# A four-layer decoder trunk on one core: TensorE in the order of emission, attention in batches

## The chip, the core and the metric

The kernel runs on one core of one Trainium2 chip. The metric is the device time of one execution in microseconds. The core has a matrix engine (TensorE, in the profile PE, with its weight loads as PEld), a vector engine (VectorE, DVE), a scalar engine (ScalarE, ACT), GpSimd (POOL) and SyncE (SP), which here issues DMAs. Each engine runs its own queue of instructions in order; semaphores tie the queues together.

## The reference

256 tokens of width 1024 go through four layers. Each layer is a token mixer and a SwiGLU feed-forward network (FFN, hidden width 2816), and each of these is wrapped in a norm before and a norm after:

```python
for i in range(DEPTH):                       # 4
    kind = i % 3
    hn = rms_norm(x, norm_gains[i, 0])
    if kind == 0:    m = diff_attention(hn, ...)            # layers 0 and 3
    elif kind == 1:  m = stick_breaking_attention(hn, ...)  # layer 1
    else:            m = sliding_window_sink_attention(hn, ...)  # layer 2
    x = x + rms_norm(m, norm_gains[i, 1])
    f = swiglu(rms_norm(x, norm_gains[i, 2]), w_gate[i], w_up[i], w_down[i])
    x = x + rms_norm(f, norm_gains[i, 3])
```

Differential attention (8 heads, rotary positions) takes two softmaxes per head, subtracts lambda times the second from the first, multiplies with the values and norms each head. Stick-breaking attention (16 heads) has sigmoids and a running product in the place of softmax. The third is attention in a window of 128 tokens with 16 query heads, 2 key heads, rotary positions and a learned sink per head. All data are float32.

## The kernel before

**Two streams.** The 256 tokens are two blocks of 128, stream 0 and stream 1 (`s`). Both run the same program, `stream(s)`, a Python generator: for each layer `pre_norm`, the mixer (`layer_a`, `layer_b` or `layer_c`), `out_proj`, `post_norm`, `pre_norm`, `ffn`, `post_norm`. A weight is read from memory once and used by both streams.

**Weight units.** The weights are cut into 378 units of 128 x 1024 numbers. A unit is loaded to a `stage` tile by a DMA on SP, then split into a high part `hi` (ScalarE) and a low part `lo` (VectorE). Every product with a weight is three matmuls of 512 columns: high with high, high with low, low with high. A unit is six such matmuls for each stream (twelve of half the width in layer 2). `RING` = 11 split units are kept; stream 0 may be at most `LAG` = 8 units ahead of stream 1; splits run `AHEAD` = 3 units ahead of stream 0. At an edge (the end of the input projection of a layer, and the end of an FFN) stream 1 goes first as long as stream 0 is past the edge and it is not.

**The emission.** The class `Emitter` runs the two streams and a list of tasks as generators and decides in which order their instructions are written down. It keeps a clock of its own, `em.t`, which goes on with each matmul by its columns times `COLUMN_NS` (four times for float32 products and transposes). A generator that yields `("d", n)` is not run again before n ns have passed on this clock; `("e", key)` waits for an event that another has set; `("w",)` takes the next weight unit. Tasks go first, then stream 0, then stream 1. If nothing can run, the clock jumps to the next time.

**Attention as tasks.** `project` multiplies a chunk (four units) of q, k or v. Each q or k chunk spawns a task `turned`: rotate (VectorE; in `layer_b` a copy on ScalarE), transpose on TensorE, copy to SBUF. After k it goes on as `scores`: two steps of score products, softmax or its like, then transposes of the weights. The task `values` multiplies with V and splits the result for `out_proj`, which waits for an event per head. A layer has two groups `g` of heads (layer 2 four tasks `heads`). In the FFN the task `turn` sends the hidden block through a transposing DMA on SP, with a copy on GpSimd before and after it (`by_dma`, `words`).

**PSUM.** Each stream has one bank tagged `tp` (transposes, values, every other FFN chunk), one tagged `mm`, and two tagged `acc` (scores, `out_proj`, the FFN's sum).

**What sets the order on the chip.** The framework's scheduler orders each engine's queue from its own forecast of times, with the order of emission as priority. Wrapped by `Start`, an instruction can be pinned behind the one before it on its engine. In the kernel before, this holds for ScalarE, VectorE, GpSimd and TensorE only up to stream 1's first norm:

```python
            if i == 0 and s:
                scalars()
                act.on = dve.on = pool.on = pe.on = False
```

Nearly all instructions carry line 182 in the profile, which is the line of this wrapper; they are told apart by tile names: `mm_f` (FFN products), `acc_f`, `acc_a`, `acc_b`, `acc_c` (sums of the FFN's second product and of `out_proj`), `mm_a000q` (layer 0, group 0: the q chunk of stream 0, from the letter of the layer, its number, the stream, the group), `tt_` (transposed q and k), `t_` (the rotated chunk), `sc_` (scores), `tw_`, `ta_`, `tpr_` (transposed weights), `pv_` (values), `to_` (transposed values), `tp_n` and `tp_q` (transposed x for the mixer's and the FFN's norm), `xh_`, `xl_` (its high and low part), `hTh_f` (high part of the transposed hidden block).

Of the kernel before, what the change touches and what calls it, by code (L numbers as in the profile page):

```python
# [38 lines left out]
COLUMN_NS = 1.0 / 2.4  # L39


class Emitter:

# [5 lines left out]
    def __init__(self, load_dma, split, n_units, edges):  # L49
        self.t = 0.0  # L50
        self.load_dma, self.split, self.n, self.edges = load_dma, split, n_units, edges
        self.issued = self.loaded = 0
        self.pos = [0, 0]
        self.ring = {}
        self.events = set()
        self.limit = 0
        self.tasks = []

# [17 lines left out]

    def run_task(self, task):
        while True:
            try:
                what = task[1].send(None)  # L80
            except StopIteration:
                return False
            if what[0] == "d":
                task[0] = self.t + what[1]
                return True
            if what[0] == "e" and what[1] not in self.events:
                task[2] = what[1]
                return True
# [35 lines left out]
    def run(self, gens):  # L124
        mains = [dict(s=s, gen=g, ready=0.0, want=None, done=False) for s, g in enumerate(gens)]
        while True:
            self.advance()
            ran = False
            for task in list(self.tasks):
                if task[2] is not None and task[2] in self.events:  # L130
                    task[2] = None
                if task[2] is None and task[0] <= self.t:
                    if not self.run_task(task):
                        self.tasks.remove(task)
                    ran = True
                    break
            if ran:
                continue

            behind = any(self.pos[1] < w <= self.pos[0] for w in self.edges)  # L140
            order = mains[::-1] if behind else mains
            if self.pos[1] == 0:
                order = sorted(order, key=lambda m: m["want"] is not None)
            for m in order:
                if self.can(m) and m["ready"] <= self.t:
                    self.run_main(m)
                    ran = True
                    break
            if ran:
                continue  # L150
            times = [x[0] for x in self.tasks if x[2] is None] + [m["ready"] for m in mains if self.can(m)]
            if not times:
                assert all(m["done"] for m in mains) and not self.tasks, "the emission is stuck"
                return
            self.t = max(self.t, min(times))
# [3 lines left out]
def trunk_kernel(ctx, tc, x, positions, norm_gains, a_w_in, a_w_out, a_lambda, a_subln, b_w_in, b_w_out,  # L159
# [9 lines left out]
    def bank(tag, s, shape, name):  # L169
        return ps.tile(shape, F32, tag=f"{tag}{s}", name=name, bufs=BANKS[tag])  # L170
# [415 lines left out]
    def layer_a(s, i, xn):  # L586
# [7 lines left out]
        def turned(chunk, g, which):  # L594
            t = rope(chunk, 8, *tabs[which], f"{name}{g}{which}")
            yield ("d", 2000)
# [3 lines left out]
            else:  # L600
                dst = qT[g] = queries(s, 4, f"{name}{g}")
            four_transposes(s, t.rearrange("p h d -> p (h d)"), dst, f"tt_{name}{g}{which}")
# [4 lines left out]
        def scores(g):  # L607
# [3 lines left out]
            yield ("d", 700)  # L611
# [4 lines left out]
            for step in range(3):  # L616
                if step < 2:
# [21 lines left out]
                    yield ("d", 3500)  # L639
                if step > 0:  # L640
                    if step == 2:
                        yield ("d", 1500)
# [5 lines left out]
                    yield ("d", 300)  # L648
# [4 lines left out]
        def values(g):  # L653
# [3 lines left out]
            yield ("d", 500)  # L657
# [12 lines left out]
            yield ("d", 4200)  # L670
# [4 lines left out]
            yield ("d", 900)  # L675
# [3 lines left out]
        for g in range(2):  # L679
            for which in "qkv":  # L680
                chunk = yield from project(s, xn, 512, 4, f"{name}{g}{which}", g == 0 and which == "q")
                if which == "v":
# [4 lines left out]
                    yield ("d", 600)  # L687
                else:
                    em.spawn(turned(chunk, g, which))
                    yield ("d", 1500)  # L690
        return oT, name

    def layer_b(s, i, xn):
# [6 lines left out]
        def turned(chunk, g, which):  # L700
            t = wk.tile([P, 512], F32, tag="t2k", name=f"t_{name}{g}{which}", bufs=TMP)
            act.activation(t, chunk, AF.Copy, scale=xn[2])
            yield ("d", 900)
# [3 lines left out]
            else:  # L707
                dst = qT[g] = queries(s, 4, f"{name}{g}")
            four_transposes(s, t, dst, f"tt_{name}{g}{which}")
# [4 lines left out]
        def scores(g):  # L714
# [3 lines left out]
            yield ("d", 700)  # L718
            aT[g] = wk.tile([P, 4, 2, nk, P], F32, tag=f"wT{s}", name=f"aT_{name}{g}", bufs=1)
            as_ = {}  # L720
            for step in range(3):
                if step < 2:
# [21 lines left out]
                    yield ("d", 3500)  # L744
                if step > 0:
                    if step == 2:
                        yield ("d", 1500)
                    for p in range(2):
                        tp = bank("tp", s, [P, 2, nk, P], f"ta_{name}{g}{2 * step - 2 + p}")
# [4 lines left out]
                        yield ("d", 300)  # L754
            em.set((name, "w", g))

        def values(g):
# [3 lines left out]
            yield ("d", 500)  # L761
# [7 lines left out]
            yield ("d", 900)  # L769
# [3 lines left out]
        for g in range(2):  # L773
            for which in "qkv":
                chunk = yield from project(s, xn, 512, 4, f"{name}{g}{which}", g == 0 and which == "q")
                if which == "v":
# [4 lines left out]
                    yield ("d", 600)  # L781
                else:
                    em.spawn(turned(chunk, g, which))
                    yield ("d", 600)
        return oT, name

    def layer_c(s, i, xn):
# [6 lines left out]
        def keys(chunk):  # L794
# [4 lines left out]
            yield ("d", 1200)  # L799
# [7 lines left out]
        def heads(chunk, g):  # L807
            t = rope(chunk, 4, *tabs["q"], f"{name}{g}q")
            yield ("d", 1300)
# [8 lines left out]
            yield ("d", 700)  # L818
# [24 lines left out]
            yield ("d", 6000)  # L843
            for p in range(2):
                tp = bank("tp", s, [P, 2, nk, P], f"tpr_{name}{g}{p}")
# [4 lines left out]
                yield ("d", 500)  # L850
# [7 lines left out]
            yield ("d", 600)  # L858
# [3 lines left out]
        for part in range(5):  # L862
# [5 lines left out]
            yield ("d", 2000)  # L868
        return oT, name

    def ffn(s, i, xn):
# [19 lines left out]
        def turn(c, h):  # L891
# [7 lines left out]
            split_rows(hT[c], slice(2 * (c % 2), 2 * (c % 2) + 2), t)  # L899
            em.set((name, "h", c))  # L900
# [19 lines left out]
        yield ("d", 700)  # L920
# [3 lines left out]
    def stream(s):  # L924
        if s:
            yield ("d", 1500)
        for i in range(depth):
            kind = i % 3
            xn = pre_norm(s, 4 * i, f"n{i}{s}")
            yield ("d", 600)  # L930
            if i == 0 and s:
                scalars()
                act.on = dve.on = pool.on = pe.on = False
# [4 lines left out]
            yield ("d", 4000)  # L938
            gain = gain_of(i, 3)
            xn = pre_norm(s, 4 * i + 2, f"q{i}{s}")  # L940
            yield ("d", 600)
            acc = yield from ffn(s, i, xn)
            post_norm(s, acc, gain, f"e{i}{s}")
            if i < depth - 1:
                yield ("d", 4000)
# [30 lines left out]
```

## Time and profile before

| | us |
|---|---|
| median of 3 runs | 1189.72 (1189.0 to 1190.4) |
| the profiled execution | 1188.92 |
| its span, first to last instruction | 1187.1 |
| PE busy | 1165.9 (98%) |
| PEld busy | 958.5 (81%) |
| DVE busy | 784.4 (66%) |
| ACT busy | 651.9 (55%) |
| POOL busy | 214.3 (18%) |

The rows that follow in the prediction come from four views. The page starts with the span and each engine's busy time. The view by stretches gives, for each stretch of the span, its length, the busy time and number of instructions of PE, PEld, DVE, ACT and POOL, the granted TensorE clock, the share of the DMA engines and GB/s. The view of waits says which instruction's engine was idle until which other was done: total us, number of times, longest. The view in order of time has start, duration, engine, line, operation, output tile and input tiles, shapes, how many were merged, and in brackets the engine's idle time before it with its releaser. Matmuls are pipelined: the next one starts before the last one's shown end.

### The profile page before, as it was taken

To read this page: it belongs to the slowest core of one execution; us is meant where nothing else is said; L and a number is where in the kernel's file an instruction comes from. 1 tells how busy PE (TensorE), PEld (TensorE's weight loads), DVE (VectorE), ACT (ScalarE), POOL (GpSimd) and SP (SyncE) were. 2 spreads that over 40 slices of the span, in tenths; PEclk is the share of its full clock that TensorE was granted. 3 is DMA by queue.
4 is the path that set the end of the run, shared out by engine and by line. 5 is a ranking of instruction groups with operands and counts; after the bars stand their busy time and mean duration, and the time that the engine had idled before them with its cause. 6 is when DMAs were issued, how large, how long until landed. Compare 5 with 4: busy or idle time off the path is not lost.

```text
span 1187.1 us, 16727 instructions
## 1 busy us (share of the span) xinstructions
PE 1165.9 (98%) x5868; PEld 958.5 (81%) x5868; DVE 784.4 (66%) x1217; ACT 651.9 (55%) x1197; POOL 214.3 (18%) x301
## 2 busy tenths in 40 slices
PE   8999999999999999999999999999999999999997
PEld 7787788888878878888888878888878788888886
DVE  7876665665847666665688666566586785666563
ACT  6665554444756655444476655445475565545442
POOL 2000132222200013222210013221210001322221
PEclk9999999999999999999999999999999999999999
DMA  7635467776743546777764246777765454677761
GB/s 280 212 122 161 146 189 222 209 213 199 239 143 125 178 143 185 216 219 209 200 214 141 90 147 195 213 210 210 207 214 154 137 175 128 177 213 214 208 194 41
DMA packets 184360, 216.41 MB, mean 182 GB/s; under 512 B 53074, under 2 KB 148436, under 8 KB 184276
## 3 DMA queue, kind: packets, MB, share of 16 engines
q1 hardware_dynamic: 183568, 215.00, 61.1%
q8 instruction: 46, 0.75, 0.3%
q10 hardware_dynamic: 708, 0.34, 0.1%
q14 instruction: 38, 0.31, 0.1%
HBM read 203.76 MB, written 1.05 MB: 173 GB/s over the span
## 4 chain that ended last, share of the span: by engine, by line
PE 90%; DVE 3%; ACT 3%; DMA 2%; issue 2%; POOL 1%; ACTq 0%; POOLq 0%; DVEq 0%; SPq 0%
PE mm_f L182 39%; PE acc_f L182 19%; PE acc_a L182 3%; PE mm_c L182 2%; PE acc_b L182 2%; PE sc_a L182 2%; PE acc_c L182 2%; DMA stage<-in_a_w_in_dram 1%; ACT hi L182 1%; DVE lo L182 1%; PE sc_c L182 1%; PE sc_b L182 1%; PE pv_a L182 1%; DVE x L182 1%; PE tp_q L182 1%
## 5 line engine op out<-in xcount | busy, mean ns | idle before, releaser
L182 DVE TENSOR_TENSOR lo<-stage,hi 128x1024 fp32r<-128x1024 f32 x378 | 459.7, 1226 | 162.0 <-ACT hi L182 159.9
L182 ACT ACTIVATE hi<-stage 128x1024 fp32r<-128x1024 f32 x378 | 394.9, 1056 | 163.3 <-PE mm_f L182 86.9
L182 PE MATMUL mm_f<-hi,xh_q 128*128 128x512 f32 x704 | 275.7, 392 | 1.5 <-ACT hi L182 1.5
L182 PE MATMUL mm_f<-lo,xh_q 128*128 128x512 f32 x704 | 274.2, 389 | 0.0
L182 PE MATMUL mm_f<-hi,xl_q 128*128 128x512 f32 x704 | 217.2, 390 | 0.4 <-DVE xl_q L182 0.4
L182 POOL COPY hp_f<-h_f 128x512 uint16<-128x512 uint16 x80 | 90.6, 1132 | 407.7 <-DVE h_f L182 393.7
L182 PEld LDWEIGHTS mm_f<-hi,xh_q 128*128 128x128 f32 x704 | 132.1, 188 | 30.5 <-ACT hi L182 3.2
L182 PEld LDWEIGHTS mm_f<-hi,xl_q 128*128 128x128 f32 x704 | 132.2, 188 | 28.7 <-DVE xl_q L182 1.2
L182 PEld LDWEIGHTS mm_f<-lo,xh_q 128*128 128x128 f32 x704 | 132.3, 188 | 26.9
L182 ACT ACTIVATE hTh_f<-hx_f 128x256 fp32r<-128x256 f32 x80 | 33.4, 418 | 166.8 <-POOL hx_f L182 166.8
L182 PE MATMUL acc_f<-hi,hTh_f 128*128 128x512 f32 x352 | 111.5, 393 | 1.2 <-ACT hTh_f L182 1.2
L182 PE MATMUL acc_f<-hi,hTl_f 128*128 128x512 f32 x352 | 109.8, 390 | 0.0
L182 PE MATMUL acc_f<-lo,hTh_f 128*128 128x512 f32 x352 | 109.8, 390 | 0.0
L182 DVE TENSOR_TENSOR hTl_f<-hx_f,hTh_f 128x256 fp32r<-128x256 f32 x80 | 33.9, 424 | 106.0 <-ACT hTh_f L182 106.0
L182 POOL COPY hx_f<-hq_f 128x512 uint16<-128x512 uint16 x80 | 81.0, 1013 | 85.6 <-DMA hq_f<-hp_f 85.1
L182 ACT ACTIVATE t_f<-mm_f,half_f 128x256 f32<-128x256 f32 x88 | 41.5, 472 | 74.4 <-PE mm_f L182 74.4
L182 PEld LDWEIGHTS acc_f<-hi,hTh_f 128*128 128x128 f32 x352 | 65.8, 188 | 15.5 <-ACT hTh_f L182 2.3
L182 PEld LDWEIGHTS acc_f<-lo,hTh_f 128*128 128x128 f32 x352 | 66.1, 188 | 13.8
L182 PEld LDWEIGHTS acc_f<-hi,hTl_f 128*128 128x128 f32 x352 | 66.0, 188 | 13.7
L182 DVE SCALAR_TENSOR_TENSOR t_f<-t_f,mm_f 128x256 f32<-128x256 f32 x88 | 36.8, 418 | 32.5 <-ACT t_f L182 32.4
L182 DVE SCALAR_TENSOR_TENSOR h_f<-t_f,hsq_f,mm_f 128x256 f32<-128x256 f32 x88 | 42.3, 480 | 2.9
L182 ACT ACTIVATE e_a<-sc_a,nm_a 128x128 f32<-128x128 f32 (+1 forms) x64 | 26.0, 420 | 17.0 <-DVE nm_a L182 16.9
(588 smaller groups left out, 1552.3 us busy)
## 6 DMA issues: line engine op xcount, KB each, us to landing
stage<-in_ffn_w_gate_dram SPq DMA_DIRECT2D x176, 256.0 KB, 3.0
stage<-in_ffn_w_up_dram SPq DMA_DIRECT2D x176, 256.0 KB, 3.3
stage<-in_ffn_w_down_dram SPq DMA_DIRECT2D x88, 512.0 KB, 4.4
stage<-in_a_w_in_dram SPq DMA_DIRECT2D x48, 512.0 KB, 4.4
stage<-in_b_w_in_dram SPq DMA_DIRECT2D x24, 512.0 KB, 4.1
stage<-in_a_w_out_dram SPq DMA_DIRECT2D x16, 512.0 KB, 3.5
stage<-in_c_w_in_dram SPq DMA_DIRECT2D x10, 512.0 KB, 4.4
gain<-in_norm_gains_dram SPq DMA_DIRECT2D x8, 512.0 KB, 4.3
```

Of the source, the lines that this page charges most:

```text
L182: i = call(*args, **kw)
```

## The change

- TensorE stays pinned to the order of emission for the whole program; the other engines are left to the scheduler as before.
- `COLUMN_NS`, the clock's cost of a matmul column, goes from 1/2.4 to 0.443 ns. Nearly all delays are new, most of them longer.
- Tasks run in batches: once no task can run any more, the next one may only run `BATCH_NS` = 2600 ns later.
- A task yields `("b", s)` before it takes a `tp` bank. If the bank of this stream was taken less than `BANK_NS` = 1200 ns ago, the task is put off until then.
- The hidden block's event in `turn` is set 1500 ns later.

No arithmetic, tile or DMA is added or removed.

```diff
-COLUMN_NS = 1.0 / 2.4
+COLUMN_NS = 0.443
+BATCH_NS = 2600
+BANK_NS = 1200
...
+        self.next_batch = 0.0
+        self.bank_free = [0.0, 0.0]
...
+    def took_bank(self, s):
+        self.bank_free[s] = self.t + BANK_NS
...
+            if what[0] == "b" and self.bank_free[what[1]] > self.t:
+                task[0] = self.bank_free[what[1]]
                 return True
...
     def run(self, gens):
+        batch = False
...
-                if task[2] is None and task[0] <= self.t:
+                if task[2] is None and task[0] <= self.t and self.t >= self.next_batch:
                     if not self.run_task(task):
                         self.tasks.remove(task)
-                    ran = True
+                    ran = batch = True
                     break
             if ran:
                 continue
+            if batch:
+                self.next_batch = self.t + BATCH_NS
+                batch = False
...
-            times = [x[0] for x in self.tasks if x[2] is None] + [m["ready"] for m in mains if self.can(m)]
+            times = [max(x[0], self.next_batch) for x in self.tasks if x[2] is None] + [m["ready"] for m in mains if self.can(m)]
...
     def bank(tag, s, shape, name):
+        if tag == "tp":
+            em.took_bank(s)
...
     def layer_a    # turned
-            yield ("d", 2000)
+            yield ("d", 2900)
+            yield ("b", s)
                    # scores
-            yield ("d", 700)
+            yield ("d", 1200)
-                    yield ("d", 3500)
+                    yield ("d", 1800 if step else 4200)
-                        yield ("d", 1500)
+                        yield ("d", 4000)
+                    yield ("b", s)
-                    yield ("d", 300)
                    # values
-            yield ("d", 500)
+            yield ("d", 1000)
+            yield ("b", s)
-            yield ("d", 4200)
+            yield ("d", 5200)
+            yield ("b", s)
-            yield ("d", 900)
+            yield ("d", 1500)
                    # after a v chunk, after a q or k chunk
-                    yield ("d", 600)
+                    yield ("d", 1000)
-                    yield ("d", 1500)
+                    yield ("d", 2200)
...
     def layer_b    # turned, scores, values, chunks
-            yield ("d", 900)
+            yield ("d", 1400)
+            yield ("b", s)
-            yield ("d", 700)
+            yield ("d", 1200)
-                    yield ("d", 3500)
+                    yield ("d", 1800 if step else 4200)
-                        yield ("d", 1500)
+                        yield ("d", 3200)
                     for p in range(2):
+                        yield ("b", s)
-                        yield ("d", 300)
+                        yield ("d", 900)
-            yield ("d", 500)
+            yield ("d", 1000)
+            yield ("b", s)
-            yield ("d", 900)
+            yield ("d", 1300)
-                    yield ("d", 600)
+                    yield ("d", 1100)
...
     def layer_c    # keys 1200 -> 1800, heads 1300 -> 2200, 700 -> 1200, 6000 -> 6500, 500 -> 900, 600 -> 1000, chunks 2000 -> 2300
...
     def ffn        # turn
             split_rows(hT[c], slice(2 * (c % 2), 2 * (c % 2) + 2), t)
+            yield ("d", 1500)
             em.set((name, "h", c))
                    # after the last chunk's transposes
-        yield ("d", 700)
+        yield ("d", 1100)
...
     def stream
             xn = pre_norm(s, 4 * i, f"n{i}{s}")
-            yield ("d", 600)
+            yield ("d", 1200)
             if i == 0 and s:
                 scalars()
-                act.on = dve.on = pool.on = pe.on = False
+                act.on = dve.on = pool.on = False
...
             post_norm(s, acc, gain, f"m{i}{s}")
-            yield ("d", 4000)
+            yield ("d", 4600)
             gain = gain_of(i, 3)
             xn = pre_norm(s, 4 * i + 2, f"q{i}{s}")
-            yield ("d", 600)
+            yield ("d", 1200)
...
             if i < depth - 1:
-                yield ("d", 4000)
+                yield ("d", 4600)
```

More of the change, by code (lines that the diff above doesn't have):

```diff
@@ L84, in run_task @@
                 task[0] = self.t + what[1]
+                return True
+            if what[0] == "b" and self.bank_free[what[1]] > self.t:
+                task[0] = self.bank_free[what[1]]
                 return True
@@ L798, in keys @@
             act.activation(V["c", s], chunk[:, P:2 * P], AF.Copy, scale=xn[2])
-            yield ("d", 1200)
+            yield ("d", 1800)
+            yield ("b", s)
             tp = bank("tp", s, [P, 2, P], f"tk_{name}")
@@ L808, in heads @@
             t = rope(chunk, 4, *tabs["q"], f"{name}{g}q")
-            yield ("d", 1300)
+            yield ("d", 2200)
+            yield ("b", s)
             tp = bank("tp", s, [P, 2, P], f"tq_{name}{g}")
@@ L842, in heads @@
                 dve.tensor_tensor(e[j], e[j], l[:, j, :].unsqueeze(2).to_broadcast([P, 2, n]), ALU.mult)
-            yield ("d", 6000)
+            yield ("d", 6500)
             for p in range(2):
+                yield ("b", s)
                 tp = bank("tp", s, [P, 2, nk, P], f"tpr_{name}{g}{p}")
@@ L849, in heads @@
                 act.activation(pT[:, p], tp, AF.Copy)
-                yield ("d", 500)
+                yield ("d", 900)
+            yield ("b", s)
             o = bank("tp", s, [P, 2, P], f"pv_{name}{g}")
@@ L857, in heads @@
             split_rows(oT[g // 2], slice(2 * (g % 2), 2 * (g % 2) + 2), o)
-            yield ("d", 600)
+            yield ("d", 1000)
             for h in range(2):
@@ L867, in layer_c @@
                 em.spawn(heads(chunk, part - 1))
-            yield ("d", 2000)
+            yield ("d", 2300)
         return oT, name
@@ L919, in ffn @@
         em.set((name, "h", c))
-        yield ("d", 700)
+        yield ("d", 1100)
         yield from down(NCH - 1)
@@ L929, in stream @@
             xn = pre_norm(s, 4 * i, f"n{i}{s}")
-            yield ("d", 600)
+            yield ("d", 1200)
             if i == 0 and s:
                 scalars()
-                act.on = dve.on = pool.on = pe.on = False
+                act.on = dve.on = pool.on = False
             gain = gain_of(i, 1)
@@ L937, in stream @@
             post_norm(s, acc, gain, f"m{i}{s}")
-            yield ("d", 4000)
+            yield ("d", 4600)
             gain = gain_of(i, 3)
             xn = pre_norm(s, 4 * i + 2, f"q{i}{s}")
-            yield ("d", 600)
+            yield ("d", 1200)
             acc = yield from ffn(s, i, xn)
```

## The prediction

> **What bounds the kernel now.** I read the page's head and part 1 first, then busy time by stage, then TensorE's waits, then three places in order of time.
>
> ```profile
> span 1187.1 us, 16727 instructions
> ...
> PE 1165.9 (98%) x5868; PEld 958.5 (81%) x5868; DVE 784.4 (66%) x1217; ACT 651.9 (55%) x1197; POOL 214.3 (18%) x301
> ```
>
> TensorE is the bound: busy for 98% of the span. Nothing in the change alters how many matmuls there are, so only its idle time can move. The next view is busy time by stretch of the span (length, then busy time of PE, PEld, DVE, ACT, POOL). I cut it at the first 17 us, the attention of layers 0, 1, 2 and 3, the start of the FFN of layer 1, and the end.
>
> ```profile
> 0.00:17.00 17.00, 12.66 (x60) 10.49 (x61) 10.96 (x29) 8.63 (x15) 4.42 (x51) 1.00 0.82 301
> 17.00:124.00 107.00, 105.07 (x577) 84.86 (x576) 81.25 (x134) 68.91 (x164) 7.77 (x12) 1.00 0.54 170
> 147.00:298.00 151.00, 151.00 (x668) 125.11 (x667) 93.52 (x122) 73.25 (x101) 40.18 (x38) 1.00 0.73 206
> 316.00:423.00 107.00, 107.00 (x655) 86.36 (x654) 69.67 (x109) 72.26 (x133) 6.54 (x24) 1.00 0.48 153
> 423.00:447.00 24.00, 22.98 (x103) 18.41 (x103) 15.10 (x24) 12.36 (x24) 2.16 (x4) 1.00 0.54 170
> 612.00:692.00 80.00, 78.11 (x630) 67.06 (x629) 63.68 (x154) 56.30 (x157) 3.31 (x8) 1.00 0.40 126
> 879.00:990.00 111.00, 109.73 (x609) 89.09 (x609) 82.16 (x147) 69.46 (x182) 7.36 (x12) 1.00 0.49 155
> 1176.00:1188.00 12.00, 4.33 (x19) 3.01 (x17) 3.15 (x5) 1.70 (x5) 0.86 (x2) 0.83 0.12 44
> ```
>
> Idle is length minus PE. The inside of an FFN has none (147 to 298), nor has the attention of layer 1 (316 to 423). Attention in layers 0, 2 and 3 idles 1.93, 1.89 and 1.27, together 5.1 us. The start of an FFN idles 1.02. The first 17 us (4.3) and the end (7.7) are not touched. So a perfect order is worth 5.1 plus some 4 to 5 us for the four FFN starts. TensorE's waits name the places:
>
> ```profile
> PE tp_q L182 <- DVE x L182: 2.5, 4, 1.2
> PE mm_f L182 <- ACT hi L182: 1.5, 4, 0.4
> ...
> PE acc_f L182 <- ACT hTh_f L182: 1.2, 4, 0.5
> ...
> PE mm_c L182 <- DVE l_c L182: 0.9, 1, 0.9
> PE mm_a300q L182 <- ACT xh_n L182: 0.9, 1, 0.9
> PE to_a L182 <- DVE on_a L182: 0.8, 1, 0.8
> PE mm_a001k L182 <- DVE t_a001q L182: 0.7, 1, 0.7
> ```
>
> The first three are the FFN starts, 5.2 in 12 waits. The other four, 3.3 us, are places where the scheduler put a matmul ahead of its input; some six smaller ones fill up the 5.1 of attention.
>
> **Part 1: the old waits in attention and between layers.** TensorE now follows the emission, and each step waits a longer delay. After stream 0's `pre_norm` the pause grows from 0.6 to 1.2 us, so stream 1's last FFN unit comes out ahead of stream 0's first product: the wait on `xh_n` at layer 3 (0.9) goes, and its twin at layer 2. Of the rest I count two thirds as gone. A busy matmul shows 0.39 us, but the next starts 0.22 to 0.23 after it (next rows), so each wait costs 0.16 more than it shows. Some ten waits are worth 5.1 + 1.6 = 6.7 at most; I take -5 and keep -3 and -6.7 as ends.
>
> **Part 2: the FFN start.** TensorE's rows in order of time when stream 1 ends `out_proj` of layer 1, and VectorE's row of its norm:
>
> ```profile
> 440.44 0.39 PE L182 MATMUL acc_b<-hi,ol_b 128*128 128x512 f32 x1
> 440.66 0.39 PE L182 MATMUL mm_f<-hi,xh_q 128*128 128x512 f32 x1
> ...
> 442.55 0.49 PE L182 MATMUL mm_f<-hi,xh_q 128*128 128x512 f32 x1 [0.37 <-ACT hi L182]
> 443.26 0.49 PE L182 MATMUL acc_f<-hi,hTh_f 128*128 128x512 f32 x1 [0.22 <-ACT hTh_f L182]
> 444.19 0.63 PE L182 MATMUL tp_q<-ident,x 128*128 128x128 f32 x4 [0.43 <-DVE x L182]
> 444.58 0.48 PE L182 MATMUL acc_f<-hi,hTh_f 128*128 128x512 f32 x1
> ```
>
> ```profile
> 443.30 1.41 DVE L182 SCALAR_TENSOR_TENSOR x<-mg_m,r_m,x 128x512 f32<-128x512 f32 x2 [1.02 <-POOL r_m L182]
> ```
>
> Stream 1 ends at 440.66; `tp_q` can take its new x 3.5 us later, at 444.19. Stream 0 is at its limit of 8 units ahead and has one unit (six matmuls, 1.36 us) left. The scheduler put three matmuls of later units into the hole (442.55, 443.26, 444.58). In the order of emission nothing of stream 0 may follow before stream 1 has taken its next unit, since no limit or edge changes: the hole keeps its length and loses three matmuls of 0.23. That is +0.7 in each of four layers, +2.7. Ends: +1 if one or two fit elsewhere, +4 if `tp_q` slips too.
>
> **Part 3: the chains of attention get longer.** This is the term that decides. A task now runs only when its delay is over and a batch opens, two units (2.72 us) after the last batch. So every step is rounded up to rounds of two units plus a batch. For stream 0's second group in layer 1, from the end of its k chunk: half a round to the first batch, transposes 1, scores 1, second scores 1.6 (4.2 us), its weights' transposes 1, 1, then 1 and 1.2 (0.9 and 3.2 us), 1, 1, values 1, done 1: 12.3 rounds, 24 to 25 units. Added up, the written delays alone rise from 12.7 to 17.7 us. Counted the same way from their delays, layers 0 and 3 come to about 11.4 rounds, layer 2 to 7.5.
>
> What can fill it: at that point stream 0 has 8 units to go to the fifth product of `out_proj`, which needs the group, and stream 1 (8 behind, first at an edge) has 12 to 16 that need nothing of this chain: 20 to 24 units, 10 to 12 rounds. So in layers 0, 1 and 3 stream 0 stands, and stream 1 spends its own first four `out_proj` units there. Those are what covers stream 0's norm today:
>
> ```profile
> 416.04 0.39 PE L182 MATMUL acc_b<-hi,ol_b 128*128 128x512 f32 x1
> 416.28 0.60 PE L182 MATMUL ta_b<-ident,b_b 128*128 128x128 f32 x4
> 416.63 0.71 PE L182 MATMUL acc_b<-hi,oh_b 128*128 128x512 f32 x2
> ...
> 419.94 1.03 PE L182 MATMUL tp_q<-ident,x 128*128 128x128 f32 x8
> 420.90 2.02 PE L182 MATMUL pv_b<-aT_b,V_b 128*64 128x128 f32 x32
> ```
>
> Between stream 0's last product (416.04) and its `tp_q` (419.94) TensorE did two units and eight transposes of stream 1 without a gap. With these units spent, up to 3 of the 3.5 us stand open, and up to 1.4 (a unit's length, my estimate) between the values and `acc_b` if both streams are dry. Layer 1: 0 to +4.4, I take +3. Layers 0 and 3: 0 to +3.2 each, +1 each, since stream 1's second scores come late there and keep its units back. Layer 2: 0 to +2, I take +1. Together +6.
>
> **Part 4: the start of layer 0.** VectorE's first and last step of the first rotated chunk:
>
> ```profile
> 19.94 0.69 DVE L182 TENSOR_TENSOR t_a000q<-mm_a000q,crq_a 128x512 f32<-128x512 f32 x1 [0.42 <-PE mm_a000q L182]
> ...
> 27.56 0.68 DVE L182 TENSOR_TENSOR t_a000q<-t_a000q 128x512 f32<-128x512 f32 x1
> ```
>
> The rotation took 8.3 us (19.94 to 28.24), and the scheduler held the transposes behind it back that long. The emission puts them 2.9 us, in units three (4.1 us), after the chunk: up to 4.2 us of wait, with everything of TensorE behind it, and VectorE's queue (weight splits between the three steps) deciding. Against it stand old waits on the same work. I take +1.5, ends -1 and +4.2.
>
> **Part 5: fewer changes of kind.** Four transposes take 0.35 (416.28 to 416.63); eight `tp_q` take 0.96 (419.94 to 420.90), 0.12 each. The 0.09 by which the next product is long is thus the transposes' own tail, not a cost of changing. Some 50 fewer changes are worth 0 to -4.5 at 0.09; I take -0.5. Hidden: `turn` issues its transposing DMA on SP, and its POOL copies, up to a round later and sets its event 1.5 us later, about 4.5 rounds in all against 6 (12 units) until the product that needs it. Without that cover each round missed would show as a wait of `acc_f` on `hTh_f`. The bank rule and COLUMN_NS add no instruction.
>
> **The sum** against the profiled execution (1188.9, its span 1187.1): -5 + 2.7 + 6 + 1.5 - 0.5 = +4.7, 1193.6. The median of the runs shown, 1189.7, stands 0.8 above that execution: 1194. All good ends give -6.7 + 1 + 0 - 1 - 4.5 = -11.2, all bad ones -3 + 4 + 12.8 + 4.2 + 0 = +18.
>
> **Rivals.** Faster: the chain of layers 0, 1 and 3 fits into 10 rounds, because a batch that lasts over 1.5 us lets the 4.2 us step pass in one round. Then stream 1 keeps its units, part 3 is 0, and with a quiet start it is -6.7 + 2.7 - 0.5 = -4.5, 1185; it decides from 20 units on. For it: layer 1 has no idle at all today, so there is some slack. Against: 12.3 rounds is far from 10.
>
> No change: gains and holes cancel, or rounding costs half of what I count (part 3 at +3, start 0): about 1190.
>
> Much slower: long holes bring the slow pace of the first microseconds back.
>
> ```profile
> 15.30 0.63 PE L182 MATMUL mm_a000q<-lo,xh_n 128*128 128x512 f32 x1
> 15.73 0.63 PE L182 MATMUL mm_a000q<-hi,xh_n 128*128 128x512 f32 x1
> ```
>
> Here matmuls start 0.43 apart, against 0.22 between 440.44 and 440.66, though the granted clock reads 1.00 in that stretch. No later wait is above 1.2 us, and none brought this pace back. If a hole of 3 us or more did, and the pace stayed halved for about as long as the hole (my estimate), that would add 2 us in each of three layers: 1200. [...]
>
> **How the numbers follow.** Chances: slower by the longer chains 0.38 (1191 to 1201), slower clock 0.06, faster 0.34 (1180 to 1187), cancelling 0.22. The likeliest gives 1194. Leaving out the best and worst tenth gives 1180 to 1204. A measurement here tells about 0.2% (2.4 us) from no change: faster 0.34, same 0.22, slower 0.44.
>
> **What would show it.** TensorE's wait of `tp_q` on x rises from 4 times to 7 or 8, and above 6 us in total; 316 to 423 idles 2 to 4 us instead of 0; the waits of `mm_c` and `mm_a300q` on `xh_n` are gone; a wait of `tt_a000q` on VectorE appears. I am wrong if layer 1's attention stays without idle time, or if the waits that I count as gone return under other names.

## The result, and the profile after

| | before | after |
|---|---|---|
| median | 1189.36 us | 1242.29 us |
| lowest to highest | 1188.77 to 1190.4 | 1241.8 to 1245.36 |
| span of the profiled execution | 1187.1 | 1240.0 |

The changed kernel is slower: ratio 1.0448, 95% interval 1.0435 to 1.0461. The page after, head and part 1:

```profile
span 1240.0 us, 16747 instructions
...
PE 1174.3 (95%) x5868; PEld 961.8 (78%) x5868; DVE 785.2 (63%) x1217; ACT 651.7 (53%) x1197; POOL 177.0 (14%) x301
```

The span grew by 52.9 us. TensorE is idle for 65.7 of it, against 21.2 before: +44.5. The same 5868 matmuls are busy 8.4 us longer, although none is new; that is the second, smaller loss. The view by stretches (length, busy time of PE, PEld, DVE, ACT, POOL, granted clock, DMA share, GB/s), cut at the attention of layers 0 to 3:

```profile
17.00:139.00 122.00, 107.79 (x581) 86.30 (x580) 83.07 (x135) 70.91 (x168) 8.43 (x12) 0.97 0.48 154
330.00:437.00 107.00, 106.33 (x628) 86.47 (x627) 69.97 (x105) 71.29 (x125) 5.83 (x24) 1.00 0.49 153
632.00:720.00 88.00, 77.35 (x605) 65.58 (x604) 60.98 (x148) 53.06 (x149) 4.95 (x8) 0.98 0.32 105
912.00:1042.00 130.00, 113.98 (x605) 92.50 (x604) 82.37 (x150) 68.75 (x169) 6.80 (x11) 0.95 0.42 130
```

Length minus PE gives the idle time: 14.2 us in layer 0, 0.7 in layer 1, 10.7 in layer 2, 16.0 in layer 3. Cut at the first product of each FFN and the last sum of each FFN, with layer 0 from 17 us on, the stages compare as follows (us, read from the start times of `mm_f` and `acc_f` in the two traces):

| | layer 0 | layer 1 | layer 2 | layer 3 | sum of differences |
|---|---|---|---|---|---|
| attention before | 107.5 | 106.9 | 76.9 | 108.1 | |
| attention after | 121.9 | 107.4 | 87.9 | 129.9 | +47.7 |
| FFN before | 191.4 | 192.8 | 189.4 | 190.3 | |
| FFN after | 190.8 | 194.8 | 192.3 | 191.2 | +5.2 |

In the three layers whose granted clock falls below 1 (0.97, 0.98, 0.95), PE's busy time in these attention stages rose too: from 105.6 to 107.7, from 75.7 to 77.4 and from 107.8 to 114.0. Layers 0, 2 and 3 rotate their q and k on VectorE; layer 1, which does not, lost 0.5. TensorE's waits after, from the view of waits (total us, times, longest):

```profile
PE tp_q L200 <- DVE x L200: 6.1, 4, 2.0
PE mm_a310v L200 <- DVE t_a310k L200: 4.6, 1, 4.6
PE mm_a311v L200 <- DVE t_a311k L200: 4.6, 1, 4.6
PE tt_a000q L200 <- DVE t_a000q L200: 4.0, 1, 4.0
PE tq_c L200 <- DVE ol_c L200: 3.5, 3, 1.4
PE mm_a301v L200 <- DVE t_a301k L200: 3.5, 1, 3.5
PE mm_f L200 <- DVE xl_q L200: 2.9, 7, 0.7
PE mm_a311k L200 <- DVE el_a L200: 2.2, 1, 2.2
...
PE mm_a001v L200 <- DVE t_a001k L200: 2.1, 1, 2.1
PE tt_a011q L200 <- DVE ol_a L200: 1.7, 1, 1.7
PE acc_f L200 <- DVE hTl_f L200: 1.6, 2, 0.8
```

Before, the longest single wait behind the first 17 us was 1.2 us. Now there are single waits (holes, below) of 4 to 5 us, and all of these rows name VectorE, which is busy for 63% of the span. Most of the long ones name a rotation, `t_a`. The first of them, in order of time, before:

```profile
28.12 0.39 PE L182 MATMUL mm_a000k<-hi,xh_n 128*128 128x512 f32 x1
28.35 0.39 PE L182 MATMUL mm_a010q<-lo,xh_n 128*128 128x512 f32 x1
28.58 0.39 PE L182 MATMUL mm_a000k<-lo,xh_n 128*128 128x512 f32 x1
...
29.26 0.60 PE L182 MATMUL tt_a000q<-ident,t_a000q 128*128 128x128 f32 x4
```

and after, TensorE and then VectorE:

```profile
23.82 0.40 PE L200 MATMUL mm_a000k<-hi,xl_n 128*128 128x512 f32 x1
28.18 1.12 PE L200 MATMUL tt_a000q<-ident,t_a000q 128*128 128x128 f32 x4 [3.96 <-DVE t_a000q L200]
28.95 0.78 PE L200 MATMUL mm_a000k<-hi,xh_n 128*128 128x512 f32 x1
29.52 0.63 PE L200 MATMUL mm_a000k<-lo,xh_n 128*128 128x512 f32 x1
29.95 0.63 PE L200 MATMUL mm_a000k<-hi,xh_n 128*128 128x512 f32 x1
```

```profile
19.32 0.69 DVE L200 TENSOR_TENSOR t_a000q<-mm_a000q,crq_a 128x512 f32<-128x512 f32 x1
...
23.44 2.35 DVE L200 TENSOR_TENSOR lo<-stage,hi 128x1024 fp32r<-128x1024 f32 x2
25.71 0.68 DVE L200 TENSOR_TENSOR t_a000q<-mm_a000q,srq_a 128x512 f32<-128x512 f32 x1
26.31 1.21 DVE L200 TENSOR_TENSOR lo<-stage,hi 128x1024 fp32r<-128x1024 f32 x1
27.44 0.68 DVE L200 TENSOR_TENSOR t_a000q<-t_a000q 128x512 f32<-128x512 f32 x1
```

Three operations of 0.7 us take 8.8 us from the start of the first to the end of the last, because weight splits and some smaller operations stand between them. Before it was 8.3 us, almost the same. What differs is TensorE: before, it went on with products of `mm_a000k` and `mm_a010q` and met the transposes (29.26) when their input was ready, without a wait. Now the transposes stand at the head of its queue, and products that have their inputs stand behind them. After the hole, matmuls start 0.43 us apart (29.52, 29.95) instead of 0.23: the slow pace returns for a while.

The second picture is from layer 3, VectorE and TensorE:

```profile
953.32 0.16 DVE L200 SCALAR_TENSOR_TENSOR os_a<-os_a,el_a 128x4 f32<-128x4 f32 x1 [1.19 <-ACT junk_a L200]
954.61 0.69 DVE L200 TENSOR_TENSOR on_a<-pv_a,os_a 128x512 f32<-128x512 f32 x1 [1.13 <-POOL os_a L200]
955.22 0.68 DVE L200 TENSOR_TENSOR t_a310k<-mm_a310k,crk_a 128x512 f32<-128x512 f32 x1
955.82 0.68 DVE L200 TENSOR_TENSOR t_a310k<-mm_a310k,srk_a 128x512 f32<-128x512 f32 x1
```

```profile
949.15 0.62 PE L200 MATMUL mm_a310k<-hi,xl_n 128*128 128x512 f32 x2
...
950.99 1.05 PE L200 MATMUL pv_a<-V_a,wT_a 128*128 128x128 f32 x8
956.64 0.77 PE L200 MATMUL mm_a310v<-hi,xh_n 128*128 128x512 f32 x1 [4.60 <-DVE t_a310k L200]
```

The chunk `mm_a310k` ends at 949.8. Its rotation begins at 955.2, because VectorE's queue first holds the norm of the values product that TensorE has just done, and that norm waits for ScalarE's squares and GpSimd's power. The next chunk needs the same `mm` bank, so TensorE waits 4.6 us.

### The profile page after: what moved, and what is told of

It is laid out like the page before. It is cut to its first block, busy times and chain, and to the rows that moved or that the text cites. A ratio compares the mean times of both kernels' runs of the same rounds, so it can differ in the third digit from the quotient of the medians.

```text
span 1240.0 us, 16747 instructions
## 1 busy us (share of the span) xinstructions
PE 1174.3 (95%) x5868; PEld 961.8 (78%) x5868; DVE 785.2 (63%) x1217; ACT 651.7 (53%) x1197; POOL 177.0 (14%) x301
## 4 chain that ended last, share of the span: by engine, by line
PE 82%; DVE 7%; ACT 4%; DMA 2%; issue 2%; POOL 2%; ACTq 0%; SPq 0%; DVEq 0%; POOLq 0%
PE mm_f L200 37%; PE acc_f L200 18%; PE acc_a L200 3%; DVE lo L200 3%; PE mm_c L200 2%; ACT hi L200 1%; PE acc_b L200 1%; PE acc_c L200 1%; PE sc_c L200 1%; PE pv_a L200 1%; DMA stage<-in_a_w_in_dram 1%; PE sc_a L200 1%; DMA gain<-in_norm_gains_dram 1%; PE mm_a311v L200 1%; PE sc_b L200 1%
## 5 line engine op out<-in xcount | busy, mean ns | idle before, releaser
L200 POOL COPY hp_f<-h_f 128x512 uint16<-128x512 uint16 x80 | 69.8, 872 | 292.9 <-DVE h_f L200 276.6
L200 POOL COPY hx_f<-hq_f 128x512 uint16<-128x512 uint16 x80 | 64.3, 804 | 243.6 <-DMA hq_f<-hp_f 243.5
L200 PEld LDWEIGHTS acc_f<-hi,hTh_f 128*128 128x128 f32 x352 | 65.8, 188 | 14.2 <-ACT hTh_f L200 0.8
```

The lines of the kernel that those rows point to most:

```text
L200: i = call(*args, **kw)
```

## The experiments

A rotation is called a rope in the expectations. Its latency is used below: from the end of a chunk's last product to the end of the rotation's last operation, 16 chunks in layers 0 and 3. Before it runs from 2.1 to 8.3 us (middle 4.0), after from 2.1 to 9.5 (middle 4.8). The delay on the emission's clock is 2.0 before and 2.9 after.

### Which part of the change costs it

My first theory T was that a batch holds back the first step of a new task, so that the rotation comes late to VectorE. Rivals: the pinning by itself (P), the longer delays (D).

`e1_nobatch`:

```diff
-BATCH_NS = 2600
+BATCH_NS = 0
```

> The changed kernel with BATCH_NS = 0: TensorE pinned, new delays and bank pauses kept, tasks emitted as soon as they are due. Theory T (the batch holds back the first step of a new task, the rope of a finished chunk; it then stands on VectorE behind work that waits for the newest values product, and pinned TensorE waits at the next chunk, which needs the same bank): most of the 52 us come back, 1190 to 1205, and no wait of an mm_a matmul on a rope over 1 us. Rival P (following the emission costs it by itself): 1230 to 1245. Rival D (the longer delays and the longer chain of attention, part 3 of the prediction): 1215 to 1235.

Measured: 1226.4, ratio 1.031 (1.0291 to 1.033). That is outside T's range, below P's and inside D's. `tt_a000q` still waits 4.0, and `mm_a010v` waits 3.4 on a rotation, which T excluded. `e3_before_pinned` and `e7_delays_only` below speak against D: pinned, the old delays are slower than the new ones, and with TensorE free the new ones cost nothing.

`e2_unpinned`:

```diff
-                act.on = dve.on = pool.on = False
+                act.on = dve.on = pool.on = pe.on = False
```

> The changed kernel with TensorE unpinned after the start (pe.on = False again): batches and delays kept, the scheduler may move matmuls past one another. Theory T: the ropes still stand late on VectorE, but TensorE's order can put other matmuls into the hole: 1205 to 1230. Rival P: 1188 to 1195. Rival D: 1225 to 1245, as the chain is as long as before.

Measured: 1195.9, ratio 1.0055 (1.004 to 1.007), just above P's range. One line takes back 46 us. One wait of the same kind is left in its trace:

```profile
PE mm_a310v L200 <- DVE t_a310k L200: 4.2, 1, 4.2
PE tp_q L200 <- DVE x L200: 1.7, 4, 0.4
```

`e3_before_pinned`, the kernel before with:

```diff
-                act.on = dve.on = pool.on = pe.on = False
+                act.on = dve.on = pool.on = False
```

> The kernel before with TensorE alone pinned: the old delays, COLUMN_NS 1/2.4, no batches. Theory T: the ropes are emitted as soon as a chunk ends, so the holes are those of delays that are a little short: 1190 to 1205. Rival P: 1230 to 1245. Rival D: 1188 to 1200.

Measured: 1235.7, ratio 1.039 (1.0372 to 1.0408), in P's range. `tt_a000q` waits 5.6 us.

`e4_first_step`, the batch rule without a task's first step:

```diff
-                if task[2] is None and task[0] <= self.t and self.t >= self.next_batch:
+                if task[2] is None and task[0] <= self.t and (self.t >= self.next_batch or not task[3]):
+                    first, task[3] = not task[3], True
...
-                    ran = batch = True
+                    ran = True
+                    batch = batch or not first
```

> The changed kernel, but the first step of a newly spawned task (rope, copy or nothing but a wait for an event) is emitted at once, whether or not a batch is open; all later steps still wait for batches. Theory T: the holes at mm_a...v, mm_a...k and tt_a...q go, with the half pace behind them: 1200 to 1215; what stays over 1190 is the longer chain in layer 2 and the FFN starts. Rival P and rival D: within 5 us of the changed kernel, 1237 to 1247.

Measured: 1245.1, ratio 1.0467 (1.0443 to 1.0492), in the range of P and D. T as the main cause falls: the rotations come out earlier, and the holes move (`tt_a001q` on `on_a` 3.8, `tt_b101q` on `ol_b` 3.7).

`e7_delays_only`, TensorE free and no batches:

```diff
-BATCH_NS = 2600
+BATCH_NS = 0
...
-                act.on = dve.on = pool.on = False
+                act.on = dve.on = pool.on = pe.on = False
```

> The changed kernel with TensorE unpinned and BATCH_NS = 0: only the longer delays, the pauses of the bank and the new COLUMN_NS are left. If the 6 us that the unpinned kernel with batches stands over the kernel before come from the batches: 1187 to 1192. If from the longer delays (part 3 of the prediction): 1193 to 1200.

Measured: 1188.6, ratio 0.9989 (0.998 to 0.9998). So with TensorE free the batches cost 7.3 us (1195.9 less 1188.6) and the delays nothing. Side by side:

| | old delays | new delays | new delays, batches |
|---|---|---|---|
| TensorE free | 1189.7 | 1188.6 | 1195.9 |
| TensorE pinned | 1235.7 | 1226.4 | 1242.3 |

Pinning costs 46, 38 and 46 us. The longer delays help the pinned kernel by 9; the batches take 16 from it.

The batches' 16 us lie mostly in layer 3, and there T describes what happens. With batches, layer 3's last five rotations have latencies of 7.0 to 7.9 us, with TensorE pinned or free (`e2_unpinned`); without batches 3.5 to 5.8 (`e1_nobatch`, `e7_delays_only`); before 2.1 to 5.2. The attention of layer 3 takes 129.9 us in the changed kernel and 118.4 in `e1_nobatch`, which is 11.5 of the 16.1 us between the two profiled executions. `e4_first_step` brings it to 120.2, but the attention of layer 1 grows there from 107.4 to 113.7 and the FFNs by 3.5 together.

`e13_batch_1300`:

```diff
-BATCH_NS = 2600
+BATCH_NS = 1300
```

> The changed kernel with BATCH_NS = 1300, half the distance between batches. If the price of the batches follows their length (0: 1226.4, 2600: 1242.3): 1230 to 1238. If it is one accident of the order at 2600: 1222 to 1229, or anything else outside.

Measured: 1225.9, ratio 1.0294 (1.028 to 1.0307), as without batches, and in the range of "one accident of the order at 2600". It does not show an accident, though: a weight unit is 1.36 us on the emission's clock (six times 512 columns at 0.443 ns), so 1300 is less than a unit and postpones little. How the price goes with the distance between batches stays open.

### A mismatch of two orders, or a tight order?

Theory M: TensorE has one order and VectorE another. Then giving all the same order should help.

`e5_all_pinned` (the flag `em.early` keeps the special first norm where it was):

```diff
-                act.on = dve.on = pool.on = False
+                em.early = False
```

> The changed kernel with VectorE, ScalarE and GpSimd also kept in the order of emission for the whole run (batches and delays as changed). Theory M (mismatch: TensorE follows the emission, while the scheduler sorts VectorE and ScalarE by its own clock, in which TensorE is elsewhere; a rope's second half then stands behind weight splits that TensorE wants later): with one order for all four engines the holes at ropes go, 1195 to 1220. Rival O (the emission's order and its delays are too tight for VectorE in itself): 1235 to 1270, with the holes at the same ropes or more of them.

Measured: 1309.1, ratio 1.0998 (1.0981 to 1.1015), 39 us above O's range.

`e6_pe_dve_pinned`:

```diff
-                act.on = dve.on = pool.on = False
+                act.on = pool.on = False
```

> The changed kernel with TensorE and VectorE in the order of emission, ScalarE and GpSimd sorted by the scheduler. Theory M: 1195 to 1225, most of the gain of pinning all four, as most of the long waits name VectorE. Rival O: 1235 to 1270.

Measured: 1311.5, ratio 1.1029 (1.1013 to 1.1044). M falls. O has the direction, but both times lie some 40 us above its range: fixing VectorE too costs another 69 us (1311.5 against 1242.3). That each fixed queue adds its own blocked heads is my reading of it. In layer 2 of `e5_all_pinned` idle time and clock are worst (same columns as above):

```profile
650.00:773.00 123.00, 87.92 (x607) 75.48 (x605) 66.29 (x153) 54.23 (x153) 3.65 (x8) 0.86 0.26 82
```

`e14_dve_alone`, as `e7_delays_only`, but:

```diff
-                act.on = dve.on = pool.on = pe.on = False
+                act.on = pool.on = pe.on = False
```

> Longer delays, no batches, and VectorE alone in the order of emission, TensorE free. With both fixed the time was 1311, with TensorE alone 1226, with neither 1188.6. If VectorE's order is what must stay free: 1250 to 1310. If TensorE, being free, goes round what VectorE brings late: 1190 to 1220.

Measured: 1236.1, ratio 1.0388 (1.0372 to 1.0403), between the two expectations. Without batches, TensorE's queue alone fixed costs 38 us against 1188.6 and VectorE's alone 48; with batches, both together cost 116 (1311.5 against 1195.9). A free TensorE goes round only part of what VectorE brings late (`mm_c` waits 6.3 us on `t_c201q`, a rotation in layer 2).

### Delays shorter than the latency

`e9_rope_delays`, pinned, no batches:

```diff
-            yield ("d", 2900)      # turned of layer_a
+            yield ("d", 6000)
-                    yield ("d", 2200)      # project of layer_a, after a chunk
+                    yield ("d", 5000)
```

> The changed kernel with BATCH_NS = 0 (1226.4) and, in the layers with ropes of 8 heads (0 and 3) alone, the delay from a finished chunk to its transposes at 6000 instead of 2900 and the pause of the stream after a chunk at 5000 instead of 2200. In the traces the last multiply of a rope ends 2.1 to 9.5 us after its chunk's last product (the middle of 16: 4.3 to 4.8). Theory V (an order fixed at one delay cannot follow a latency that varies by a factor of four; where the delay is shorter, TensorE stands): the holes at t_a are covered, 1203 to 1216. Rival L (the longer chain then breaks elsewhere, at scores, weights or values): 1220 to 1240.

Measured: 1212.3, ratio 1.0187 (1.0169 to 1.0206), as V had it. `tt_a000q` waits 1.0 instead of 4.0, and the attention of layer 0 idles 2.5 us in 107, near the 1.9 before. Layer 2, whose delays were left, still idles 11.2:

```profile
17.00:124.00 107.00, 104.51 (x587) 84.93 (x586) 82.56 (x136) 70.09 (x167) 8.26 (x12) 1.00 0.55 176
617.00:706.00 89.00, 77.79 (x611) 66.25 (x610) 60.17 (x147) 52.62 (x150) 3.76 (x8) 0.96 0.31 101
```

`e15_pinned_long`, on top of that:

```diff
-BANK_NS = 1200
+BANK_NS = 3000
...
-            yield ("d", 1800)      # keys of layer_c
+            yield ("d", 5000)
-            yield ("d", 2200)      # heads of layer_c
+            yield ("d", 5000)
-            yield ("d", 2300)      # project of layer_c
+            yield ("d", 4500)
...
-            yield ("d", 4600)      # between post_norm and the FFN's pre_norm
+            yield ("d", 6500)
...
-            yield ("d", 1200)      # after the FFN's pre_norm
+            yield ("d", 2200)
```

> TensorE pinned, no batches, the long delays at the ropes of layers 0 and 3 (1212.3 so far), and longer delays at the other places where TensorE still stands: layer 2's chunks 5000 for 1800 and 2200 and 4500 for 2300, the pause of a transpose bank 3000 for 1200, the start of an FFN 6500 and 2200 for 4600 and 1200. If the loss is delays shorter than the latency: 1195 to 1207. If the longer chain breaks elsewhere: 1209 to 1230.

Measured: 1213.1, ratio 1.0194 (1.0181 to 1.0207): no gain, in the range of the longer chain that breaks elsewhere. Layer 2 loses the waits of `tk_c` and gets others (its stretch still idles 8.8 of 89 us), and layer 1 gets a wait of 3.5 us (`tt_b101q` on `ol_b`). Delays alone did not bring a pinned TensorE back; 23 us stayed.

`e12_rope_delays_free`, `e9_rope_delays` with TensorE free:

```diff
-                act.on = dve.on = pool.on = False
+                act.on = dve.on = pool.on = pe.on = False
```

> The same long delays at the ropes of layers 0 and 3 (6000 and 5000) and no batches, with TensorE free (the free kernel without them: 1188.6). If a longer chain of attention costs time in itself, as part 3 of the prediction has it: 1191 to 1200. If the scheduler lays other work beside it: 1183 to 1189; the low end if the hole of 3 us before mm_a010v of that kernel goes.

Measured: 1185.1, ratio 0.9956 (0.9943 to 0.9969): faster than both kernels. The same delays, which in the fixed order left 23 us, are here only priorities. Its rows at the place shown above, TensorE and VectorE:

```profile
28.75 0.39 PE L200 MATMUL mm_a000k<-lo,xh_n 128*128 128x512 f32 x1
28.98 0.60 PE L200 MATMUL tt_a000q<-ident,t_a000q 128*128 128x128 f32 x4
```

```profile
25.74 0.68 DVE L200 TENSOR_TENSOR t_a000q<-mm_a000q,srq_a 128x512 f32<-128x512 f32 x1
26.34 0.67 DVE L200 TENSOR_TENSOR t_a010q<-mm_a010q,crq_a 128x512 f32<-128x512 f32 x1
26.94 0.67 DVE L200 TENSOR_TENSOR t_a000q<-t_a000q 128x512 f32<-128x512 f32 x1
```

The rotation ends at 27.6, as late as ever, and TensorE has no wait. By stages (the cuts of the table above) attention differs from before by -2.0, +1.8, -2.5 and +4.6 us, the FFNs by -2.5, -2.5, +0.8 and -1.5: against the kernel before, the gain lies in the FFN stages. `e7_delays_only` has most of that already; what `e12_rope_delays_free` gains on it lies in the attention of layer 0, 105.5 instead of 109.3, where the hole of 3 us is gone.

### Ropes, or what stands before them

`e10_rope_one_op` in the changed kernel and `e11_before_rope_one_op` in the one before:

```diff
-        dve.tensor_tensor(t1, bv, cr.unsqueeze(1).to_broadcast([P, n, 64]), ALU.mult)
...
-        dve.tensor_tensor(t2.rearrange("p h (a d) -> p h a d", a=2), b4, s4, ALU.mult)
         for o in (outs or [t1]):
-            dve.tensor_tensor(o, t1, t2, ALU.add)
+            dve.tensor_tensor(o, bv, cr.unsqueeze(1).to_broadcast([P, n, 64]), ALU.mult)
```

> The changed kernel with a rope of one multiply by the cosine in place of two multiplies and an addition: the sine's part is left out. TensorE's work and order are as in the changed kernel. If the ropes on VectorE make the holes: those that name t_a (some 25 us of waiting and 8 of half pace behind it in the changed kernel) mostly go, 1205 to 1220. If the ropes only stand at the end of other late work on VectorE (weight splits, the norm of the values): 1228 to 1240.

> The kernel before with the same rope of one multiply (the sine's part left out), as the comparison for the run with it in the changed kernel. TensorE is the bound there and waits on ropes for 2 us in all: 1185 to 1190 by every theory.

Measured: 1225.5, ratio 1.0303 (1.0287 to 1.0318), between the two expectations, and 1184.4, ratio 0.9957 (0.9942 to 0.9972; 0.6 below its range). The rope's own length is worth 16.8 us in the changed kernel and 4.8 in the one before, so some 12 of the 53. The wait in layer 3 hardly moved, 3.9 instead of 4.6: what counts there is the work ahead of the rope.

`e16_values_off_dve` (pinned, batches) and `e17_free_values_off` (the same with TensorE free):

```diff
-            dve.scalar_tensor_tensor(ss, ss, 1.0 / P, st[g, "el"], ALU.mult, ALU.add)
+            pool.tensor_scalar(ss, ss, 1.0 / P, None, ALU.mult)
+            pool.tensor_tensor(ss, ss, st[g, "el"], ALU.add)
...
-            dve.tensor_tensor(on, o, ss.unsqueeze(2).to_broadcast([P, 4, P]), ALU.mult)
+            for h in range(4):
+                act.activation(on[:, h, :], o[:, h, :], AF.Copy, scale=ss[:, h:h + 1])
```

> The changed kernel (1242.3) with the norm of the values taken off VectorE: os_a as two small GpSimd instructions in place of one on VectorE, on_a as four ScalarE copies with a scale in place of one multiply on VectorE. The order of TensorE is unchanged. If VectorE's queue, standing at os_a and on_a with ropes behind them, makes the holes before mm_a310v and mm_a311v (4.6 us each, some 4.2 us of half pace behind them) and part of those before mm_a301v and mm_a311k: 1222 to 1232. If the next late instruction takes their place, 1237 to 1247.

Measured: 1235.8, ratio 1.039 (1.0373 to 1.0407), between the two.

```profile
PE mm_f L200 <- DVE xl_q L200: 3.8, 7, 1.9
...
PE tt_a011q L200 <- DVE ol_a L200: 2.9, 1, 2.9
...
PE tt_a311q L200 <- DVE rl_a L200: 1.6, 1, 1.6
...
PE mm_a311v L200 <- DVE t_a311k L200: 1.4, 1, 1.4
PE mm_a310v L200 <- DVE t_a310k L200: 1.4, 1, 1.4
```

The two waits fell from 4.6 to 1.4 each, and the slow pace behind them is gone; so VectorE's blocked queue made them. Others grew: `tt_a011q` from 1.7 to 2.9, `mm_f` from 2.9 to 3.8, and `tt_a311q` is new.

> The same edit in the changed kernel with TensorE free and batches on (1195.9 without the edit; one hole of 4.2 us before mm_a310v with 2.5 us of half pace behind it makes up nearly all that it stands over the free kernel without batches, 1188.6). If that hole is the price of the batches: 1186 to 1191. If the batches cost through something else: 1193 to 1197.

Measured: 1194.8, ratio 1.0044 (1.0029 to 1.0059). The hole before `mm_a310v` fell from 4.2 to 1.0, but `acc_a` now waits 2.2 on `e_a` and `to_a` 2.6 on `on_a`. That one hole is not the whole price of the batches. Against `e7_delays_only` the rest is spread over the stages, at most 2.8 us in one of them (the attention of layer 2); what makes it up stays open.

`e18_best_values_off`, the same edit in `e12_rope_delays_free`:

```diff
-            dve.tensor_tensor(on, o, ss.unsqueeze(2).to_broadcast([P, 4, P]), ALU.mult)
+            for h in range(4):
+                act.activation(on[:, h, :], o[:, h, :], AF.Copy, scale=ss[:, h:h + 1])
```

> The fastest kernel so far (TensorE free, no batches, long delays at ropes: 1185.0) with the same edit. Its trace has 2.5 us of holes at on_a and the rope behind it (to_a, mm_a310v). If they go: 1181 to 1184. If ScalarE's four copies come later than VectorE's one multiply: 1185 to 1189.

Measured: 1187.3, ratio 0.9979 (0.9969 to 0.9988): ScalarE's copies come later than VectorE's multiply (`to_a` waits 4.9 us in four places, where it waited 1.7 in one).

### The start of the FFN

`e8_ffn_edge`, in the kernel before:

```diff
+        edges.append(len(units))
         for c in range(NCH):
             gate_up(i, c)
```

> The kernel before with one more edge, after the last unit of each layer's output projection, so that stream 1 catches up there before stream 0 begins its FFN. If stream 1's last units then cover stream 0's norm and stream 0's first units cover stream 1's, the FFN starts (5.2 us in 12 waits) shrink: 1184 to 1188. If the scheduler had filled that place already: 1188 to 1192.

Measured: 1192.5, ratio 1.0023 (1.0014 to 1.0032), above both expectations. By stages the FFNs get shorter by 1.6, 9.0, 4.7 and 1.7 and attention longer by 3.7, 9.4, 6.6 and 1.8: work of stream 1 moves into the attention stages, and more is lost there than the FFNs gain.

## Why the prediction was wrong

The direction was right, 1194 against 1242 was not. The sum forecast +4.7; the span grew by 52.9. That the sign came out right is luck: the term that was to decide, part 3 in layer 1, did not come, and the one that did decide stood in the sum as a gain.

**The step that failed** is the first sentence of part 1, with what I drew from it: "TensorE now follows the emission, and each step waits a longer delay." I priced the pinning by the waits that the free kernel still had (5.1 us) and took it as a gain of 3 to 6.7. The price was the waits that the scheduler avoided, and no wait row of the profile before shows these. Pinning alone cost 46 us (`e3_before_pinned`); with it, the new delays gave back 9 and the batches took 16, together 52.6. The row that would have told it was quoted in part 4: a rotation of 8.3 us against a delay of 2.0. I used it at the start of layer 0 alone; the latencies of the 16 rotations, 2.1 to 8.3 us with a middle of 4.0, were in the trace.

**Part 1** (-5): the waits on `xh_n` are gone, as said; 1.6 us of `acc_f` on `hTl_f` stand in their place, the same sum as the 0.9 and 0.7 before. Of the others that I named, `to_a` on `on_a` and `mm_c` on `l_c` are gone too, and `mm_a001k` on `t_a001q` is longer, 1.3 instead of 0.7. The old waits thus mostly went as forecast; the loss is waits that were not there before.

**Part 2** (+2.7): +5.2 over the four FFN stages. Of these 1.6 are the waits of `acc_f` just named, at the end of two FFNs, which the term did not mean; 3.6 are left, near the bad end of 4. `tp_q` waits 6.1 instead of 2.5. With TensorE pinned and no batches it is 5.4 (`e1_nobatch`, `e9_rope_delays`), with all queues free and the new delays 1.4 to 1.7, so most of it is the pinning, as the step had it.

**Part 3** (+6): wrong in mechanism and place. Layer 1, for which I took +3, lost 0.5: the chain of 12.3 rounds found enough work beside it. Layers 0 and 3, +1 each, lost 14.4 and 21.8, and layer 2, +1, lost 11.0, mostly by waits inside the attention and not by a stream that ran dry. Longer delays with TensorE free cost nothing (`e7_delays_only`) or gain (`e12_rope_delays_free`). That the batches cost 7.3 us in the free kernel is near my +6 only in size: of the 9.8 us between the two profiled executions, 5.4 lie in the attention of layer 3, which is not where I had it.

**Part 4** (+1.5): `tt_a000q` waits 4.0, close to the bad end of 4.2, and the slow pace behind it was not in the term.

**Part 5** (-0.5): too small to be told in these runs. `turn` stayed hidden: the two waits of `acc_f` on `hTl_f` stand at the end of an FFN (630 and 910 us), whose last chunk does not go through it.

**The rival "much slower"** (1200, chance 0.06) had the second mechanism right: long holes do bring the slow pace back. In the changed kernel PE's busy time grew by 8.4 us, as the same matmuls ran slower behind the holes: 34 pairs of 512-column matmuls start 0.43 us apart there, and none in the kernel before, both counted behind the first 20 us. I tied it to three holes of 3 us and had no account of where more would come from. No row of the kernel before shows after what length of hole the pace turns slow: it is slow there up to 16.5 us, and the longest idle time ahead of that is 1.35 us, before the first `mm_a000q`.

**What would show it:** `tp_q` went above 6 us in total, but in 4 waits, not 7 or 8. The waits on `xh_n` are gone and `tt_a000q` appears, as said. Layer 1 idles 0.7 us, not 2 to 4, which I had named as the sign that I am wrong.

What stays open: which delay or wait makes the pinned kernel's last 23 us (in `e9_rope_delays` attention stands +11.7 in layer 2, +7.0 in layer 3 and +3.2 in layer 1 above the kernel before, and `e15_pinned_long` did not bring it down), and what the batches cost beside the late rotations of layer 3.

## What to carry to other kernels

In this kernel, fixing the order of the busiest engine turned every delay in the emission from a priority into a promise: each time another queue was later than promised, all work behind it stood. Before pinning, compare the delays with the spread of the latencies that the trace shows, not with the waits that are left: the waits that a scheduler avoids stand in no view. The longer delays were worth having, but as priorities: with TensorE left free and no batches, those of the change gave 1188.6, and with the ropes' delays lengthened further 1185.1.

## What the runs showed of the hardware

I had not expected the slow pace after holes as short as some of these. Over all executions profiled here I took TensorE's idle stretches (holes) of 0.6 us and more behind the first 20 us, and of these the ones with at least five pairs of 512-column matmuls that start within 4.5 us of the hole's end. After 35 of 38 holes of 3.3 us and more at least two pairs started 0.43 us apart instead of 0.23, after 21 of 35 between 1.9 and 3.3, after 2 of 12 between 1.6 and 1.9, after 3 of 218 below 1.6. In the changed kernel alone it was after all 4 of 3.3 us and more (3.48, 3.96, 4.59 and 4.60 us), after 1 of 3 between 1.9 and 3.3 (after 2.14 us, not after 2.02 and 2.23) and after none of the 19 shorter ones; the pace stayed slow for 5 to 14 matmuls.

Transposes stand beside many of the shorter holes, so the time without a 512-column product is often longer than the hole. They do not explain all of them: holes of 2.23 us with no transpose beside them were followed by the slow pace in `e1_nobatch` and `e13_batch_1300`, and by the usual pace in the changed kernel, all before `mm_a311k`. What decides there stays open.
